# Six of eight groups of an MLP's first half computed transposed, with operands at chosen places

## The chip, the cores and the metric

The kernel runs on one core of a Trainium2 chip. The metric is device time in microseconds (us), from a run's first to its last instruction with what the launch adds around it; lower is better. Engines are named as the profile names them: PE (matrix unit, its weight loads apart as PEld), DVE (vector), ACT (scalar and activation), POOL, and SP, which here only issues DMAs.

## The reference

A decoder trunk of two layers on 256 tokens of 1024 features, float32, batch 1. Each layer is a mixer and an MLP, each between two RMS norms with gains:

```python
for layer in range(2):
    h = rms_norm(x, norm_mix_pre[layer])
    m = mixer_a(h, ...) if layer == 0 else mixer_c(h, ...)
    x = x + rms_norm(m, norm_mix_post[layer])
    h = rms_norm(x, norm_mlp_pre[layer])
    x = x + rms_norm(sq_relu_mlp(h, mlp_w1[layer], mlp_w2[layer]), norm_mlp_post[layer])

def sq_relu_mlp(h, w1, w2):          # w1: 1024 x 4096, w2: 4096 x 1024
    h = jax.nn.relu(h @ w1)
    return (h * h) @ w2
```

Mixer A is a gated short convolution beside latent attention with 8 heads; mixer C is sparse attention with 16 heads in three branches. Both start with a wide input projection and end with an output projection. For the change the MLP matters, and of the mixers only where their matmul operands lie.

## The kernel before, in words

**Precision.** A float32 product is built from three matmuls on rounded operands: both factors are split into a high part, rounded to the format that PE multiplies fast, and a low part, the rest; high x high, high x low and low x high are summed in PSUM (`mm3`, L119). Weights come by DMA in chunks of 128 x 1024 (512 KB, tile `raw`); `chunk` (L158) lets ACT copy the high part (`whi`, L177, two halves of 512) and DVE subtract for the low part (`wlo`, L178). Five chunk buffers (`WB`) hold split weights; a side pool of three (`xhi`, `xlo`) takes the first chunks of the next stage. All this runs ahead of PE.

**A group** (`group_steps`, L199) is 512 output columns. The activations stand: for a token tile t (two of 128 tokens) and a slice kt of 128 features, the 128x128 block of x transposed (`xth`, `xtl`) is loaded as weights, and 512 columns of `whi` or `wlo` move through. 8 slices x 3 products = 24 matmuls per token tile, first all of t = 0, then all of t = 1: "half groups" below. Tokens lie on PSUM's partitions.

**The MLP** (`mlp`, L340). The first half has 8 groups (j = 0 to 7). When a half group ends, `epi_for` (L346) lets ACT apply ReLU with the token's 1/rms as scale (tile `hr`, L349), DVE square it (`hs`, L351), and, 3.5 us later by the planner's clock, PE transpose it in four blocks of 128x128 (`tr`, L111), since the second half needs the hidden values with their features on the partitions. ACT copies the high part from PSUM (`hh`, L359), DVE subtracts for the low one (`hl`, L360). The second half (`two_sided`, L305) has 32 slices of 128 hidden features, 2 column groups and 2 token tiles: 32 x 2 x 2 x 3 = 384 matmuls of 512 columns, `hh` and `hl` standing. `finish` (L273) then computes the norm behind it (ACT `sq` L278, DVE `pst` L280, POOL `rp` L147), adds to X (L287) and sets off the transposes of X for the next stage (`transposed`, L255), which make the four `xth`/`xtl` pairs, one per token tile and half of the features.

**What sets the order.** PE's order is fixed by the program: a small planner (`tick`, `defer`, L74 to L89) adds an estimate per matmul to a clock and lets deferred work, such as transposes and attention heads, into PE's stream when it comes due. The other engines' orders are a scheduler's; they work in order, each instruction waiting by semaphores. DMAs are all issued by SP.

**Places.** By the addresses that the build gives to the tiles, modulo 128 bytes (a standing block and its moving columns; difference = standing minus moving; "within 512" where it tells more):

| stage, matmul width | moving | standing | difference |
|---|---|---|---|
| MLP first half, 512 | whi, wlo: 64 | xth, xtl: 0 | 64 |
| MLP second half, 512 | whi, wlo: 64 | hh, hl: 64 | 0 (0 within 512) |
| a_in, c_in (input projections), c_out, 512 | whi, wlo: 64; xhi, xlo: 96 | xth, xtl: 0 | 64; 32 |
| a_out, 512 | whi, wlo: 64 | 96 | 32 |
| a_kv 512, a_qup 384 | whi, wlo: 64 | 32 | 96 |
| a_c, first use of 256 | xhi, xlo: 96 | 0 | 32 |
| c_v1, 256 | whi, wlo: 64 | 0 | 64 |
| scores in mixer C, 256 or 512 | kTh, kTl: 96 | qT: 96 | 0 (384 within 512) |

Of the kernel before, what the change touches and what calls it, by code (L numbers as in the profile page):

```python
# [17 lines left out]
P = 128  # L18
# [25 lines left out]
FILL = (900.0, 1400.0, 1200.0, 800.0, 900.0, 1200.0, 900.0, 900.0, 1000.0, 1100.0, 1300.0, 1400.0)  # L44


class Pairs:


    def __init__(self, tiles, t, q):  # L50
        self.tiles, self.t, self.q = tiles, t, q

    def __getitem__(self, key):
        i = 4 * self.q + key[1]
        return self.tiles[i // 2][:, 2 * (i % 2) + self.t, :]


class Trunk:
# [43 lines left out]

    def mm(self, ps, a, b, start, stop, passes=1):
        self.nc.tensor.matmul(ps, a, b, start=start, stop=stop)  # L104
        n = 1
        for d in b.shape[1:]:
            n *= d
        self.tick(passes * max(25.0, n / 2.4 + 2.5))
# [45 lines left out]

    def close_extra(self):
        self.xs.close()

# [82 lines left out]

    def xt_tile(self, part):
        return self.mp.tile([P, 4, P], F32R, name="xt" + part, tag="xt" + part, bufs=4)

# [10 lines left out]

    def transposed(self, src, gcols, res, q, new=None, n=4):  # L255

        new = new or self.xt_tile
        h, l = new("h"), new("l")
# [13 lines left out]

    def finish(self, t, ps, ms, cg, gp, idx, x, rx):  # L273

        nc = self.nc
        with self.tc.high_priority():
            sl = slice(cg * 512, (cg + 1) * 512)
            nc.scalar.activation(self.scratch("sq"), ps, AF.Square, scale=1.0 / 32.0, accum_out=ms[:, cg:cg + 1])  # L278
            tmp = self.scratch("pst")
            nc.vector.tensor_tensor(tmp, ps, gp[:, sl], op=OP.mult)  # L280
            self.tmp.append(tmp)
            if cg == 0:
                return
            r = self.rstd_of((ms[:, 0:1], ms[:, 1:2]), EPS, "rp")
            for i in range(2):
                sl = slice(i * 512, (i + 1) * 512)
                nc.vector.scalar_tensor_tensor(self.X[t][:, sl], self.tmp.pop(0), r, self.X[t][:, sl],  # L287
                                               OP.mult, OP.add)
# [50 lines left out]

    def mlp(self, layer, x, rx, fin):  # L340
        nc, A = self.nc, self.A
        with self.pool("hid") as hp:
            gp = self.gain_post(2 * layer + 1)
            hid = [[None] * 8 for _ in range(2)]

            def epi_for(j):  # L346
                def epi(t, ps):
                    r = hp.tile([P, 512], F32, name="hr", tag="hr", bufs=2)
                    nc.scalar.activation(r, ps, AF.Relu, scale=self.rxof(rx, t))  # L349
                    s = hp.tile([P, 512], F32, name="hs", tag="hs", bufs=3)  # L350
                    nc.vector.tensor_tensor(s, r, r, op=OP.mult)  # L351

                    def later():
                        pt = self.trp()
                        for i in range(4):
                            self.tr(pt[:, i, :], s[:, i * P:(i + 1) * P])
                        h = hp.tile([P, 4, P], F32R, name=f"hh{t}_{j}")
                        l = hp.tile([P, 4, P], F32R, name=f"hl{t}_{j}")
                        nc.scalar.activation(h, pt, AF.Copy)  # L359
                        nc.vector.tensor_tensor(l, pt, h.bitcast(F32), op=OP.subtract)  # L360
                        hid[t][j] = (h, l)
                    self.defer(3500.0, later)
                return epi

            self.first_two(self.group_steps(x, f"w1_{layer}", 0, 8, 512, epi_for(0), 0, cs=self.ahead),
                           self.group_steps(x, f"w1_{layer}", 1, 8, 512, epi_for(1), 1))
            for j in range(2, 8):
# [5 lines left out]
            self.two_sided(hid, f"w2_{layer}", 32, lambda *a: fin(*a, gp),  # L373
                           ahead=ahead if layer == 0 else None)


    def mixer_a(self, x, rx, fin):
        nc, A = self.nc, self.A
        with ExitStack() as st:
# [17 lines left out]
            with self.pool("lc") as cpool:  # L397
                cqs = [cpool.tile([P, 768], F32, name=f"cqs{t}") for t in range(2)]
                ckvs = [cpool.tile([P, 256], F32, name=f"ckvs{t}") for t in range(2)]
                cms = [cpool.tile([P, 4], F32, name=f"cms{t}") for t in range(2)]  # L400
                ckvT = [[None], [None]]
                seen = [0]

                def ctile(n):
                    def new(part):
                        seen[0] += 1
                        return cpool.tile([P, n, P], F32R, name=f"ct{part}{seen[0]}")
                    return new
# [216 lines left out]
    def mixer_c(self, x, rx, fin):  # L625
        nc, A = self.nc, self.A
        with ExitStack() as st:
            lp = st.enter_context(self.pool("ca"))
            pp = st.enter_context(self.pool("caps", space=PSUM))
            cbias = lp.tile([P, 2, C_HEADS, 16], F32, name="cbias")  # L630
            has = lp.tile([P, 2], F32, name="has")
            kTh = lp.tile([P, GRP, 2, 2, P], F32R, name="kTh")
# [6 lines left out]
            qT = [[None] * 4 for t in range(2)]  # L639
            gates = [lp.tile([P, 3, C_HEADS], F32, name=f"gates{t}") for t in range(2)]  # L640
            rq = [None, None]
# [145 lines left out]

            mixT = [[None, None], [None, None]]
            ready, out_ps, out_cs = {}, {}, {}
# [126 lines left out]
            def pv_(n):  # L916
                for _ in range(min(n, len(pvq))):
# [7 lines left out]
                    if last:  # L925
                        mh, ml = self.xt_tile("h"), self.xt_tile("l")
                        m2 = mh.rearrange("p a b -> p (a b)")
                        y = yps[gp, t]
                        nc.scalar.activation(m2, y, AF.Copy)
                        nc.vector.tensor_tensor(ml.rearrange("p a b -> p (a b)"), y, m2.bitcast(F32),  # L930
                                                op=OP.subtract)
                        mixT[t][gp] = (mh, ml)
# [69 lines left out]
    def start(self, x):  # L1002
# [7 lines left out]
        for _ in range(WARM):  # L1010
            nc.tensor.matmul(ps, warm[:, 0:P], warm, start=True, stop=True)
        hs, ls = [], []
        for t in range(2):
            for q in range(2):
                x[t][q] = Pairs(hs, t, q), Pairs(ls, t, q)
        with self.pool("init") as ip:
            raw = ip.tile([P, 8, 2, P], F32, name="x0r")

            def part(i):
                sl = slice(2 * i, 2 * i + 2)  # L1020
                nc.sync.dma_start(raw[:, sl], A["xT"][:, sl])
                h, l = self.xt_tile("h"), self.xt_tile("l")
                hs.append(h)
                ls.append(l)
                self.split_scaled_([(h[:, 2 * k:2 * k + 2], l[:, 2 * k:2 * k + 2], raw[:, 2 * i + k],
                                     self.cols[:, 2 * i + k:2 * i + k + 1]) for k in range(2)])
            part(0)
# [6 lines left out]
            cs.append(self.chunk(W[0, 3], 2, 512))  # L1034
        c2 = []
        for t in range(2):
            c2.append(self.chunk(A["a_c"][0, t], 4, 256, extra=True))
# [6 lines left out]
    def run(self):  # L1044
# [11 lines left out]
        with self.tc.manual_schedule(engines={mybir.EngineType.PE}):  # L1056
            for layer in range(2):
                for part in range(2):
                    idx = 2 * layer + part + 1
                    nx, nrx = [[None, None], [None, None]], [None, None]  # L1060

                    def fin(t, ps, ms, cg, gp, idx=idx, nx=nx, nrx=nrx):
                        self.finish(t, ps, ms, cg, gp, idx, nx, nrx)
                    if part == 1:
                        self.mlp(layer, x, rx, fin)
# [4 lines left out]
                    x, rx = nx, nrx  # L1070

# [102 lines left out]
```

## Time and profile before

| what | value |
|---|---|
| median of 3 runs | 653.75 us (653.66 to 654.86) |
| the profiled execution | 654.89 us, its span 652.9 us |
| granted clock of PE, mean | 0.994 |
| busy: PE, PEld, DVE, ACT, POOL | 638.5, 515.8, 417.7, 382.8, 77.8 us |
| matmuls and weight loads | 3150 each |
| moved by DMA | 110.04 MB, mean 169 GB/s |

In the span, layer 0's mixer ends at about 129 us, its MLP at 309; layer 1's mixer at 461, its MLP at 653. How to read it: a row of the chain of waits or of the timeline gives start, length, engine, line, tiles (out <- in) and count; a row of groups gives count, busy us, mean ns, then the idle time before and what ended it. Matmuls overlap, so the pace of a stream is the distance between starts, or a chain piece's length over its count, and not the length of one matmul's record (0.39 us for 512 columns, 0.28 us for 256). A few per cent of the records can be missing.

### The profile page before, as it was taken

The page shows a single profiled execution, that of the slowest core. Times are in us where ns is not written, and L with a number is a line of the kernel's source. Part 1 is how long each engine was busy: PE and PEld are TensorE (multiplying, and loading weights), DVE is VectorE, ACT ScalarE, POOL GpSimd, SP SyncE. Part 2 cuts the span into 40 slices and gives each one's busy share as a digit, 9 for nine tenths or more (in the row PEclk, how much of TensorE's full clock was granted, in tenths as well). Part 3 has the DMA queues.
Part 4 walks back from the last instruction along what each step waited for, and adds up shares of the span by engine and source line. Part 5 has one row for each costly group of instructions (what it writes and reads, how often), then busy time and mean ns, then how long its engine had stood idle before and what let it go on. Part 6 is the DMA issues. An engine that isn't in the chain of part 4 may idle for free.

```text
span 652.9 us, 9401 instructions
## 1 busy us (share of the span) xinstructions
PE 638.5 (98%) x3150; PEld 515.8 (79%) x3150; DVE 417.7 (64%) x963; ACT 382.8 (59%) x866; POOL 77.8 (12%) x135
## 2 busy tenths in 40 slices
PE   8999999999999999999999999999999999999995
PEld 4889877788888888888889876566788888888884
DVE  6668798766657654447748787754965665644443
ACT  4886566746556544446737778765855655644431
POOL 1202340020000000000200155640200000000000
PEclk9999999999999999999999999989999999999998
DMA  8856346545644665556615734012645565655521
GB/s 274 285 188 224 110 123 204 204 141 161 194 162 162 202 212 195 195 184 237 209 34 162 261 102 155 33 65 79 212 141 181 160 192 165 211 194 194 192 79 64
DMA packets 32608, 110.04 MB, mean 169 GB/s; under 512 B 4080, under 2 KB 4656, under 8 KB 32560
## 3 DMA queue, kind: packets, MB, share of 16 engines
q1 hardware_dynamic: 32560, 109.44, 51.3%
q8 instruction: 25, 0.41, 0.3%
q14 instruction: 23, 0.19, 0.1%
HBM read 108.38 MB, written 1.05 MB: 168 GB/s over the span
## 4 chain that ended last, share of the span: by engine, by line
PE 93%; DVE 2%; issue 1%; ACT 1%; DMA 1%; SPq 0%; POOL 0%; DVEq 0%; POOLq 0%; ACTq 0%
PE acc L104 80%; PE tr L111 6%; PE sc L104 5%; DMA raw<-in_a_in 1%; PE tr L116 1%; PE yp L104 1%; ACT pbn L875 1%; DVE xlo L178 0%; DVE wlo L178 0%; ACT pt L899 0%; DVE X L287 0%; POOL rp L147 0%; DVE pbn L873 0%; DVE pst L280 0%; ACT whi L177 0%
## 5 line engine op out<-in xcount | busy, mean ns | idle before, releaser
L178 DVE TENSOR_TENSOR wlo<-raw,whi 128x512 fp32r<-128x512 f32 (+3 forms) x368 | 236.3, 681 | 99.6 <-ACT whi L177 96.4
L177 ACT ACTIVATE whi<-raw 128x512 fp32r<-128x512 f32 (+3 forms) x362 | 205.7, 614 | 106.9 <-PE acc L104 103.2
L104 PE MATMUL acc<-whi,xtl 128*128 128x512 f32 (+3 forms) x416 | 163.5, 393 | 0.0
L104 PE MATMUL acc<-whi,xth 128*128 128x512 f32 (+3 forms) x416 | 161.9, 389 | 0.1
L104 PE MATMUL acc<-wlo,xth 128*128 128x512 f32 (+3 forms) x416 | 160.6, 387 | 1.1 <-DVE wlo L178 1.1
L104 PE MATMUL acc<-whi,hl 128*128 128x512 f32 x256 | 100.0, 391 | 0.0
L104 PE MATMUL acc<-wlo,hh 128*128 128x512 f32 x256 | 99.6, 389 | 0.0
L104 PE MATMUL acc<-whi,hh 128*128 128x512 f32 x256 | 99.6, 389 | 0.0
L104 PEld LDWEIGHTS acc<-whi,xth 128*128 128x128 f32 x416 | 78.5, 189 | 17.4 <-issue 2.8
L104 PEld LDWEIGHTS acc<-wlo,xth 128*128 128x128 f32 x416 | 78.2, 188 | 17.8 <-DVE wlo L178 2.4
L104 PEld LDWEIGHTS acc<-whi,xtl 128*128 128x128 f32 x416 | 78.6, 189 | 14.4
L104 PEld LDWEIGHTS acc<-wlo,hh 128*128 128x128 f32 x256 | 48.1, 188 | 10.0
L104 PEld LDWEIGHTS acc<-whi,hl 128*128 128x128 f32 x256 | 48.1, 188 | 9.9
L104 PEld LDWEIGHTS acc<-whi,hh 128*128 128x128 f32 x256 | 48.1, 188 | 9.8
L147 POOL TENSOR_TENSOR rp<-mse,mhalf 128x1 f32<-128x1 f32 x8 | 4.8, 597 | 405.3 <-DVE mse L144 405.3
L359 ACT ACTIVATE hh<-tr 128x512 fp32r<-128x512 f32 x32 | 19.1, 598 | 48.6 <-PE tr L111 48.6
L360 DVE TENSOR_TENSOR hl<-tr,hh 128x512 fp32r<-128x512 f32 x32 | 22.1, 692 | 38.5 <-ACT hh L359 38.5
L880 POOL TENSOR_SCALAR pbn<-pbn,sm,gates 128x128 f32<-128x128 f32 (+1 forms) x64 | 37.3, 593 | 77.3 <-DVE sm L877 74.5
L351 DVE TENSOR_TENSOR hs<-hr 128x512 f32<-128x512 f32 x32 | 22.0, 688 | 17.3 <-ACT hr L349 17.3
L875 ACT ACTIVATE pbn<-pbn,nm 128x128 f32<-128x128 f32 (+1 forms) x64 | 28.5, 448 | 7.7 <-DVE nm L873 5.9
L349 ACT ACTIVATE hr<-acc,rx 128x512 f32<-128x512 f32 x32 | 22.0, 688 | 18.6 <-PE acc L104 17.4
L873 DVE CUSTOM_DVE_ANT_0 pbn<-sc,bias 128x128 f32<-128x128 f32 (+1 forms) x64 | 21.2, 348 | 3.3 <-PE sc L104 3.0
(234 smaller groups left out, 777.4 us busy)
## 6 DMA issues: line engine op xcount, KB each, us to landing
raw<-in_w SPq DMA_DIRECT2D x128, 512.0 KB, 3.5
raw<-in_c_in SPq DMA_DIRECT2D x16, 512.0 KB, 4.0
raw<-in_a_in SPq DMA_DIRECT2D x15, 512.0 KB, 4.7
raw<-in_a_out SPq DMA_DIRECT2D x8, 512.0 KB, 3.7
raw<-in_c_out SPq DMA_DIRECT2D x8, 512.0 KB, 3.3
raw<-in_a_qup SPq DMA_DIRECT2D x6, 384.0 KB, 3.5
gpost<-in_gpost SPq DMA_DIRECT2D x4, 512.0 KB, 4.8
bias<-in_bias SPq DMA_DIRECT2D x4, 512.0 KB, 5.7
```

The costliest lines, as they stand in the source:

```text
L104: self.nc.tensor.matmul(ps, a, b, start=start, stop=stop)
L111: self.nc.tensor.transpose(dst, src, self.ident)
L116: self.nc.tensor.transpose(dst.bitcast(F32R), src, self.ident_r)
L177: nc.scalar.activation(hi[:, sl], raw[:, sl], AF.Copy)
L178: nc.vector.tensor_tensor(lo[:, sl], raw[:, sl], hi[:, sl].bitcast(F32), op=OP.subtract)
L349: nc.scalar.activation(r, ps, AF.Relu, scale=self.rxof(rx, t))
L351: nc.vector.tensor_tensor(s, r, r, op=OP.mult)
L359: nc.scalar.activation(h, pt, AF.Copy)
L360: nc.vector.tensor_tensor(l, pt, h.bitcast(F32), op=OP.subtract)
L873: nc.vector.tensor_tensor_reduce(pb[:, sl], sp[:, sl], bias[:, r, 256 - nk:], -1.0, BIG, OP.add, OP.min, nm[:, br:br + 1])
L875: nc.scalar.activation(pb[:, sl], pb[:, sl], AF.Exp, bias=nm[:, br:br + 1], scale=-1.0, accum_out=sm[:, br:br + 1])
L880: nc.gpsimd.tensor_scalar(pb[:, sl], pb[:, sl], sm[:, br:br + 1], gates[t][:, 1 + br, h:h + 1], OP.mult, OP.mult)
```

## The change

Groups 2 to 7 of each MLP's first half are computed transposed (`hidden_steps`): a 128x128 block of `w1` stands, and both token tiles move, 2 x 128 = 256 columns. Hidden features then lie on PSUM's partitions, which is what the second half needs, so these groups have no transposes. A group is 4 chunks x 4 blocks of hidden features x 2 slices x 3 products = 96 matmuls of 256 columns into two PSUM tiles of 512, chunk after chunk, so that each chunk is used once and for both token tiles. `epi_turned` takes a PSUM tile (two blocks, both token tiles) through ReLU, square, high copy and low difference, all 512 wide; high and low parts are now read from SBUF, reordered so that token tiles stand apart.

The 1/rms of a token is a scale per partition only where tokens lie on partitions. So it leaves the ReLU in all eight groups: as relu(r a)^2 = r^2 relu(a)^2 for r > 0, its square `r2` is applied in `finish`, in the square's scale and in the multiplication with the gain, now a scalar_tensor_tensor.

To move both token tiles, `xth` and `xtl` hold both in one tile (`xt_both`), three buffers of 1056 instead of four of 512. The offset of 16 elements in the MLPs (`16 if idx in (1, 3)`) puts these operands 64 bytes past a multiple of 128; some tiles in the pools are padded (`even`, and small tiles made wider), so that every other operand of a rounded matmul starts at a multiple of 128. By the build's addresses:

| stage, width | difference now |
|---|---|
| turned groups, 256 | 64 |
| MLP groups 0 and 1, 512 | 64 as before |
| MLP second half, 512 | 0 (0 within 512) as before |
| a_in, a_kv, a_out, c_in, c_out, 512 | 0 (0, 128, 256 and 384 within 512) |
| a_c, c_v1, a_b, a_qup, 256 to 384 | 0 |
| rounded transposes in mixer C, 128 | 0 (were 96) or 64 (were 32) |

The diff, cut to its core:

```diff
@@ trunk helpers
-    def mm(self, ps, a, b, start, stop, passes=1):
-        self.nc.tensor.matmul(ps, a, b, start=start, stop=stop)
+    def mm(self, ps, a, b, start, stop, passes=1, part=False):
+        self.nc.tensor.matmul(ps, a, b, start=start, stop=stop, **({"skip_group_check": True} if part else {}))
+    def even(self, pool, n):
+        pool.tile([P, n], F32, name="even")
     def close_extra(self):
+        self.even(self.xp, 24)
         self.xs.close()
-    def xt_tile(self, part):
-        return self.mp.tile([P, 4, P], F32R, name="xt" + part, tag="xt" + part, bufs=4)
+    def xt_tile(self, part, off=0):
+        x = self.mp.tile([P, 1024 + 32], F32R, name="xt" + part, tag="xt" + part, bufs=3)
+        return x[:, off:off + 1024].rearrange("p (t i n) -> p t i n", t=2, i=4)
+    def xt_both(self, both, q, t, off=0):
+        if both[q] is None:
+            both[q] = self.xt_tile("h", off), self.xt_tile("l", off)
+        return [a[:, t] for a in both[q]]
@@ finish
-            nc.scalar.activation(self.scratch("sq"), ps, AF.Square, scale=1.0 / 32.0, accum_out=ms[:, cg:cg + 1])
-            nc.vector.tensor_tensor(tmp, ps, gp[:, sl], op=OP.mult)
+            if r2 is None:
+                ...
+            else:
+                nc.scalar.activation(self.scratch("sq"), ps, AF.Square, scale=r2[t][:, 1:2], accum_out=ms[:, cg:cg + 1])
+                nc.vector.scalar_tensor_tensor(tmp, ps, r2[t][:, 0:1], gp[:, sl], OP.mult, OP.mult)
...
-                        x[t], i))
+                        x[t], i, lambda: self.xt_both(both, i, t, 16 if idx in (1, 3) else 0)))
@@ mlp
+    def hidden_steps(self, both, wname, j, epi):
+        cs = self.chunks(wname, j, range(4), 2, 512)
+        ps = [self.acc(i).rearrange("p (a n) -> p a n", a=2) for i in range(2)]
+        for c in range(4):
+            for a in range(4):
+                o = ps[a // 2][:, a % 2]
+                for i in range(2):
+                    kt = 2 * c + i
+                    xh, xl = (m[:, :, kt % 4, :] for m in both[kt // 4])
+                    wh, wl = (w[:, i, a * P:(a + 1) * P] for w in cs[c])
+                    first = kt == 0 and a % 2 == 0
+                    last = kt == 7 and a % 2 == 1
+                    self.mm(o, wh, xh, first, False, part=True)
+                    self.mm(o, wh, xl, False, False, part=True)
+                    self.mm(o, wl, xh, False, last, part=True)
+                if c == 3 and a % 2 == 1:
+                    epi(a // 2, ps[a // 2])
-                    nc.scalar.activation(r, ps, AF.Relu, scale=self.rxof(rx, t))
+                    nc.scalar.activation(r, ps, AF.Relu)
+            def epi_turned(j):
+                ...
+                def epi(b, ps):
+                    r = hp.tile([P, 512], F32, name="hr", tag="hr", bufs=2)
+                    nc.scalar.activation(r, ps.rearrange("p a n -> p (a n)"), AF.Relu)
+                    s = hp.tile([P, 512], F32, name="hs", tag="hs", bufs=3)
+                    nc.vector.tensor_tensor(s, r, r, op=OP.mult)
+                    s4 = s.rearrange("p (a t n) -> p a t n", a=2, t=2)
+                    hb, lb = h[:, 2 * b:2 * b + 2], l[:, 2 * b:2 * b + 2]
+                    nc.scalar.activation(hb, s4, AF.Copy)
+                    nc.vector.tensor_tensor(lb, s4, hb.bitcast(F32), op=OP.subtract)
...
+            for t in range(2):
+                r = self.rxof(rx, t)
+                r2[t] = self.small(2, "r2")
+                nc.vector.tensor_tensor(r2[t][:, 0:1], r, r, op=OP.mult)
+                nc.vector.tensor_scalar(r2[t][:, 1:2], r2[t][:, 0:1], 1.0 / 32.0, None, OP.mult)
             for j in range(2, 8):
-                self.group(x, f"w1_{layer}", j, 8, 512, epi_for(j), j)
+                self.hidden_steps(both, f"w1_{layer}", j, epi_turned(j))
@@ mixers: tiles made wider, and the mixed heads in a tile for both token tiles
-            uT = lp.tile([P, 4, 2 + S], F32, name="uT")
+            uT = lp.tile([P, 4, 8 + S], F32, name="uT")
-            has = lp.tile([P, 2], F32, name="has")
+            has = lp.tile([P, 32], F32, name="has")[:, 0:2]
...
```

Two places show the order of the instructions. The first is PE in the first half of layer 0's MLP, group 2, second token tile, before (out <- moving, standing; a number tells buffers apart; L104 is a matmul, L111 four transposes of the half group before):

```order
L104 MATMUL acc0_1921<-whi_1869,xth_1672 128x512
L104 MATMUL acc0_1921<-wlo_1870,xth_1672 128x512
L104 MATMUL acc0_1921<-whi_1869,xtl_1673 128x512
L104 MATMUL acc0_1921<-whi_1869,xth_1672 128x512
L104 MATMUL acc0_1921<-wlo_1870,xth_1672 128x512
L111 MATMUL tr_1939<-ident_70,hs_1919 128x128 x4
L104 MATMUL acc0_1921<-whi_1869,xtl_1673 128x512
```

and now, at the end of group 2 and the beginning of group 3:

```order
L93 MATMUL acc1_1887<-xth_1585,wlo_1881 128x256
L93 MATMUL acc1_1887<-xth_1585,whi_1880 128x256
L93 MATMUL acc1_1887<-xtl_1586,whi_1880 128x256
L93 MATMUL acc1_1887<-xth_1585,wlo_1881 128x256
L93 MATMUL acc0_2039<-xth_1567,whi_2009 128x256
L93 MATMUL acc0_2039<-xtl_1568,whi_2009 128x256
L93 MATMUL acc0_2039<-xth_1567,wlo_2010 128x256
```

Operands have changed sides, 24 matmuls of 512 became 48 of 256, and no transposes of hs stand between them; 32 sets of four stood there in both layers together, 8 are left (groups 0 and 1).

The second place is ACT at the end of group 2 in the changed kernel (L397 is the ReLU of a PSUM tile, L402 the high copy, L171 the weight copies):

```order
L397 ACTIVATE hr_1981<-acc0_1886 128x512
L402 ACTIVATE hh_2_1852<-hs_1983 128x512
L397 ACTIVATE hr_1999<-acc1_1887 128x512
L171 ACTIVATE whi_2153<-raw_2151 128x512 x2
L402 ACTIVATE hh_2_1852<-hs_2001 128x512
L171 ACTIVATE whi_2161<-raw_2159 128x512 x2
L171 ACTIVATE whi_2169<-raw_2167 128x512 x2
L171 ACTIVATE whi_2177<-raw_2175 128x512 x2
L397 ACTIVATE hr_2125<-acc0_2039 128x512
```

The ReLU of acc1_1887 waits for the last matmul of group 2. The chunk copied right behind it, whi_2153, is the first of group 4: all four of group 3 are copied before. In the kernel before, one ReLU stood at the end of each half group, with two or four weight copies between.

More of the change, by code (lines that the diff above doesn't have):

```diff
@@ L363, in epi_for @@
                 return epi
+            def epi_turned(j):
+                h = hp.tile([P, 4, 2, P], F32R, name=f"hh_{j}")
+                l = hp.tile([P, 4, 2, P], F32R, name=f"hl_{j}")
+                def epi(b, ps):
[8 more added lines that the diff above has]
+                    for t in range(2):
+                        hid[t][j] = (h[:, :, t], l[:, :, t])
+                return epi
             self.first_two(self.group_steps(x, f"w1_{layer}", 0, 8, 512, epi_for(0), 0, cs=self.ahead),
                            self.group_steps(x, f"w1_{layer}", 1, 8, 512, epi_for(1), 1))
+            for t in range(2):
+                r = self.rxof(rx, t)
+                r2[t] = self.small(2, "r2")
+                nc.vector.tensor_tensor(r2[t][:, 0:1], r, r, op=OP.mult)
+                nc.vector.tensor_scalar(r2[t][:, 1:2], r2[t][:, 0:1], 1.0 / 32.0, None, OP.mult)
             for j in range(2, 8):
-                self.group(x, f"w1_{layer}", j, 8, 512, epi_for(j), j)
+                self.hidden_steps(both, f"w1_{layer}", j, epi_turned(j))
             def ahead():
@@ L372, in ahead @@
                 self.ahead = self.chunks("c_in", 0, range(4), 2, 512, extra=XB)
-            self.two_sided(hid, f"w2_{layer}", 32, lambda *a: fin(*a, gp),
+            self.two_sided(hid, f"w2_{layer}", 32, lambda *a: fin(*a, gp, r2),
                            ahead=ahead if layer == 0 else None)
@@ L399, in mixer_a @@
                 ckvs = [cpool.tile([P, 256], F32, name=f"ckvs{t}") for t in range(2)]
-                cms = [cpool.tile([P, 4], F32, name=f"cms{t}") for t in range(2)]
+                cms = [cpool.tile([P, 32], F32, name=f"cms{t}") for t in range(2)]
                 ckvT = [[None], [None]]
@@ L404, in ctile, with new @@
                 def ctile(n):
-                    def new(part):
+                    def new():
                         seen[0] += 1
-                        return cpool.tile([P, n, P], F32R, name=f"ct{part}{seen[0]}")
+                        return [cpool.tile([P, n, P], F32R, name=f"ct{part}{seen[0]}") for part in "hl"]
                     return new
@@ L639, in mixer_c @@
             qT = [[None] * 4 for t in range(2)]
-            gates = [lp.tile([P, 3, C_HEADS], F32, name=f"gates{t}") for t in range(2)]
+            gates = [lp.tile([P, 4, C_HEADS], F32, name=f"gates{t}")[:, 0:3] for t in range(2)]
             rq = [None, None]
@@ L925, in pv_ @@
                     if last:
[L926 to L931, printed above, removed]
+                        mh, ml = self.xt_both(mixed_, gp, t)
+                        y = yps[gp, t].rearrange("p (a b) -> p a b", a=4)
+                        nc.scalar.activation(mh, y, AF.Copy)
+                        nc.vector.tensor_tensor(ml, y, mh.bitcast(F32), op=OP.subtract)
                         mixT[t][gp] = (mh, ml)
@@ L1011, in start @@
             nc.tensor.matmul(ps, warm[:, 0:P], warm, start=True, stop=True)
-        hs, ls = [], []
+        both = [[self.xt_tile(part) for part in "hl"] for _ in range(2)]
         for t in range(2):
             for q in range(2):
-                x[t][q] = Pairs(hs, t, q), Pairs(ls, t, q)
+                x[t][q] = [a[:, t] for a in both[q]]
         with self.pool("init") as ip:
@@ L1021, in part @@
                 nc.sync.dma_start(raw[:, sl], A["xT"][:, sl])
[L1022 to L1026, printed above, removed]
+                self.split_scaled_([tuple(a[:, :, 2 * (i % 2) + k] for a in both[i // 2])
+                                    + (raw[:, 2 * i + k], self.cols[:, 2 * i + k:2 * i + k + 1]) for k in range(2)])
             part(0)
@@ L1035, in start @@
         c2 = []
+        self.even(self.mp, 16)
         for t in range(2):
```

30 lines of the change are left out of this document (13 added, 17 removed).

## The prediction

> **What bounds the kernel now.** I read the page's shares first, then the chain of work that ended last, then the two MLPs in a table of stages, then single instructions of TensorE.
>
> ```profile
> PE 638.5 (98%) x3150; PEld 515.8 (79%) x3150; DVE 417.7 (64%) x963; ACT 382.8 (59%) x866; POOL 77.8 (12%) x135
> PEclk9999999999999999999999999989999999999998
> ...
> PE 93%; DVE 2%; issue 1%; ACT 1%; DMA 1%; SPq 0%; POOL 0%; DVEq 0%; POOLq 0%; ACTq 0%
> ```
>
> A busy share of 98% proves little where matmuls overlap; that 93% of the chain is TensorE, at the full clock, does. Time is won where the stream of matmuls gets shorter. The stages of the MLPs (columns: stretch, its us, busy time and count of PE, PEld, DVE, ACT, POOL, clock, DMA share, GB/s):
>
> ```profile
> 149.40:221.80 72.40, 72.40 (x338) 58.60 (x337) 46.03 (x73) 41.70 (x72) 0.00 (x0) 1.00 0.55 175
> 227.80:308.70 80.90, 80.90 (x358) 66.71 (x356) 42.01 (x67) 37.74 (x68) 1.20 (x4) 1.00 0.62 209
> ...
> 484.00:557.00 73.00, 73.00 (x342) 59.41 (x341) 46.62 (x74) 41.86 (x74) 0.00 (x0) 1.00 0.56 174
> ```
>
> The first row is twelve half groups of the first half of layer 0's MLP, the last the same in layer 1, the middle one the second half. ACT and DVE are busy for under two thirds. The chain in order of time (start, us, what) says how a half group is spent:
>
> ```profile
> 149.47 5.60 PE acc L104 x24
> 155.50 5.60 PE acc L104 x24
> 161.54 5.60 PE acc L104 x24
> ...
> 227.82 80.94 PE acc L104 x357
> ```
>
> Each half group is 24 matmuls of 512 columns in 5.60 us, **233.3 ns** each, and the next begins 6.03 us after the last began: 0.43 us go to something else. The last row is the second half: the same width, the same clock, but 80.94/357 = **226.7 ns** each. The 0.43 us are the transposes (start, us, instruction):
>
> ```profile
> 202.94 0.39 PE L104 MATMUL acc<-wlo,xth 128*128 128x512 f32 x1
> 203.17 0.60 PE L111 MATMUL tr<-ident,hs 128*128 128x128 f32 x4
> 203.52 0.48 PE L104 MATMUL acc<-whi,xtl 128*128 128x512 f32 x1
> 203.84 0.39 PE L104 MATMUL acc<-whi,xth 128*128 128x512 f32 x1
> ```
>
> The four take 0.35 us of the order, and the matmul behind them holds the stream 0.32 us in place of 0.23.
>
> **Part 1, the transposes.** Groups 2 to 7 no longer have them: 6 groups x 2 token tiles x 2 layers = 24 sets, x 0.43 us = **-10.4 us**. Groups 0 and 1 keep theirs. Nothing hid these: they lie in the stream that sets the end.
>
> **Part 2, the turned matmuls.** Removed: 12 groups x 48 = 576 at 233.3 ns, 134.4 us. Added: 12 x 96 = 1152 of 256 columns, each with a weight load of its own. So 116.7 ns is even; what does one cost? Streams of that width stand in the mixers, at their beginning and end:
>
> ```profile
> 19.88 0.28 PE L104 MATMUL acc<-xhi,xth 128*128 128x256 f32 x1
> ...
> 24.02 0.28 PE L104 MATMUL acc<-xhi,xtl 128*128 128x256 f32 x1
> ```
>
> These are 36 matmuls, 35 steps in 4.14 us: 118.3 ns. Their operands lie 32 bytes apart within 128. Another group, 64 bytes apart as the new ones will be:
>
> ```profile
> 372.65 0.28 PE L104 MATMUL acc<-whi,xth 128*128 128x256 f32 x1
> ...
> 373.59 0.28 PE L104 MATMUL acc<-whi,xtl 128*128 128x256 f32 x1
> ...
> 374.99 0.28 PE L104 MATMUL sc<-kTh,qT 128*128 128x256 f32 x1
> 375.11 0.28 PE L104 MATMUL sc<-kTl,qT 128*128 128x256 f32 x1
> 375.23 0.28 PE L104 MATMUL acc<-whi,xth 128*128 128x256 f32 x1
> ...
> 375.70 0.28 PE L104 MATMUL acc<-wlo,xth 128*128 128x256 f32 x1
> ...
> 376.50 0.28 PE L104 MATMUL acc<-whi,xtl 128*128 128x256 f32 x1
> ```
>
> Its first stretch runs at 0.94/8 = 117.5 ns, its last at 0.80/7 = 114.3. The two score matmuls between them read their moving operand in two pieces of 128 columns, as the new ones do (one per token tile), and take 0.12 us, so the cut costs little. I take **114.5 ns**, by the last stretch: the new streams are 96 long and may settle as this one did. That is 131.9 us, **-2.5 us**. The upper bound is the two pieces' 120 ns (138.2 us, +3.8). For the lower: 256 further columns cost at most 226.7 - 114.3 = 112 ns, and a 256-wide matmul without any fixed part takes that (129.0 us, -5.4).
>
> **Part 3, places.** By the build's addresses every operand pair of the second half lies at one place within 128 bytes, now as then, so its 226.7 ns should stay. The first half's lie 64 apart, the mixers' mostly 64 or 32, and all of those run at 233:
>
> ```profile
> 33.94 5.59 PE acc L104 x24
> ...
> 472.38 6.99 PE acc L104 x30
> ```
>
> that is 232.9 ns in layer 0's input projection (64) and 233.0 in the first groups of layer 1's MLP (64). I know nothing else that divides the two paces: load on ACT and DVE is alike in the stages above. The change brings 600 matmuls of 512 columns to one place: 192 of a_in, 24 of a_kv, 96 of a_out, 192 of c_in, 96 of c_out. At 6.6 ns that is 4.0 us if all set the end. In the head stages (96 in layer 0, 144 in layer 1) TensorE also waits for softmax:
>
> ```profile
> 369.00:450.00 81.00, 76.70 (x434) 55.65 (x435) 54.76 (x240) 60.87 (x192) 37.29 (x64) 0.98 0.28 93
> ```
>
> so I count half of these 240, and not the first 36, which wait for their weights: 444 x 6.6 = 2.9 us. I give back 0.3 for narrower matmuls and the rounded transposes, whose places move too with no row that says which way. **-2.6 us**, between 0 (places do nothing, or only a match within 512 bytes helps, which the second half alone has) and -4.0.
>
> The Trainium skill, "TensorE: Matmul & The Clock Gate", section "Step-by-step: what each phase is for", speaks against this part: it says that TensorE has two independent read ports and that "Loading the next tile's weights doesn't steal SBUF read bandwidth from the running matmul". By that rule places cost nothing and part 3 is 0. The trace does not decide it: 226.7 against 233.3 ns at one width and clock speaks for places, but only one stage shows the fast pace.
>
> **Part 4, ACT, DVE and the wait.** A half group leaves these behind, in their own rows:
>
> ```profile
> L360 DVE TENSOR_TENSOR hl<-tr,hh 128x512 fp32r<-128x512 f32 x32 | 22.1, 692 | 38.5 <-ACT hh L359 38.5
> L351 DVE TENSOR_TENSOR hs<-hr 128x512 f32<-128x512 f32 x32 | 22.0, 688 | 17.3 <-ACT hr L349 17.3
> ...
> L349 ACT ACTIVATE hr<-acc,rx 128x512 f32<-128x512 f32 x32 | 22.0, 688 | 18.6 <-PE acc L104 17.4
> ```
>
> Four steps per half, before and after; the copy of the high part now reads SBUF, as the weight copy does:
>
> ```profile
> L177 ACT ACTIVATE whi<-raw 128x512 fp32r<-128x512 f32 (+3 forms) x362 | 205.7, 614 | 106.9 <-PE acc L104 103.2
> ```
>
> so the work on either engine stays within 1 us a layer, and 46.03 of 72.40 us leaves room even if the stage shrinks to 66. The results are ready some 2.7 us after a half (four such rows); the earliest use is the second half of the MLP, and group 7's first use lies 336 matmuls later. The scale by 1/rms moves out of the ReLU into the end of the MLP as one squared factor: four DVE instructions of one column per layer, and at the end a multiplication with one scalar more; the row of that form there takes 1.41/2 = 0.70 us against 0.69 now:
>
> ```profile
> 641.37 0.69 DVE L280 TENSOR_TENSOR pst<-acc,gpost 128x512 f32<-128x512 f32 x1 [2.09 <-ACT sq L278]
> 642.84 1.41 DVE L287 SCALAR_TENSOR_TENSOR X<-pst,rp,X 128x512 f32<-128x512 f32 x2 [0.66 <-POOL rp L147]
> ```
>
> All of that I count at 0. It is hidden by the matmul stream but for the last multiplication. The new wait: on ACT the ReLU of a group's second half stands until TensorE ends the group, and the weight conversions behind it stand too. The order shows that the first of these is a chunk of the group after the next; four chunks, a whole group of 96 x 114.5 ns = 11.0 us, are converted ahead. Without that lead each of the twelve groups would stand for a ReLU, a copy and a subtraction (0.688 + 0.614 + 0.69 = 2.0 us), 24 us in all. DMA must bring a chunk of 512 KB in 2.75 us in place of 3.0; the second half already takes one every 12 x 226.7 ns = 2.72 us, at 209 GB/s.
>
> **The sum.** -10.4 - 2.5 - 2.6 + 0 = -15.5 us. The profiled execution took 654.89 us (span 652.9 and 2.0 around it), 1.14 above the median of the runs shown, 653.75. 653.75 - 15.5 = **638.3 us**.
>
> **The rivals.**
>
> *Places do nothing* (or not at these distances). Then part 3 is 0 and the new stream runs like the quoted stretches on average, 117 ns (134.8 us, +0.4): -10.0, **643.8 us**. For it: the fast pace stands in one stage alone, where operands also match within 512 bytes, and stretches 64 apart ran at 117.5. Against: the 6.6 ns hold through 80 us of it.
>
> *Weight loads come to light.* The loads double in number for the same columns, and the record of one is longer than 114 ns:
>
> ```profile
> L104 PEld LDWEIGHTS acc<-whi,xth 128*128 128x128 f32 x416 | 78.5, 189 | 17.4 <-issue 2.8
> ```
>
> If a long stream fell to one matmul per 189 ns, it would be 1152 x 189 = 217.7 us: +83.3 in place of -2.5, **724 us**. It decides from (134.4 + 10.4 + 2.6)/1152 = 128 ns on: from there the change is slower. Against it: 36 matmuls in a row at 118.3 with the same loads.
>
> *Weights come late.* The lead on ACT melts because copies wait for DVE at the head of the queue: up to 24 us, 638.3 + 24 = **662 us**; from 15.5/12 = 1.3 us a group on nothing is left. Against it: the lead of 11 us and a third of ACT idle.
>
> *Given back.* TensorE arrives earlier in the mixers and waits there longer for softmax, the norms or DMA; a third to two thirds of the gain is lost: about **649 us**.
>
> That the change doesn't do what it says I exclude: the order shows the 24 sets gone and 1152 matmuls in.
>
> **How the numbers follow.** Forecast 60%, own range 634 to 641.5 (parts 2 and 3 at their bounds don't meet); places nothing 27%; weight loads 3%; weights late 5%; given back 5%. The range of 8 in 10, **634 to 647**, holds most of the first two and half of the last. A measurement of this kernel tells about 0.2% (1.3 us) from no change. Faster: 60 + 27 + 5 + 1 of the late weights = 93%; the same 2%; slower 5%.
>
> **What would show it.** The transposes of hs at 32 instead of 128; chain pieces of w1 without 0.43 us gaps; a turned group in 96 x 114.5 = 11.0 us (11.3 with the first rival, over 12.3 if loads show); 226.7 ns in the second half still, and the same in a_in, a_out and c_in if places count, 233 if not. TensorE waiting for whi or wlo at a group's start would be the late weights. I am wrong if the turned stream takes over 120 ns a matmul, or if the mixers' stages grow.

## The result and the profile after

The changed kernel takes **644.34 us** (median of 4 runs, 643.85 to 645.70) beside 654.31 (653.66 to 655.77) for the kernel before on the same chip: ratio 0.9846, 95% interval 0.9824 to 0.9867, so 8.7 to 11.5 us faster. The forecast was 638.3. The time is inside the range of 8 in 10 (634 to 647), outside the likeliest case's own range (634 to 641.5), and within 0.6 us of the first rival's 643.8. As the experiments show, it got there for another reason than that rival's.

The page after, shares and the end of the chain:

```profile
PE 626.1 (98%) x3630; PEld 532.5 (83%) x3630; DVE 418.2 (65%) x971; ACT 379.7 (59%) x866; POOL 78.0 (12%) x135
...
PE 63%; issue 28%; DVE 4%; ACT 2%; DMA 2%; POOL 1%; SPq 0%; DVEq 0%; POOLq 0%; ACTq 0%
```

TensorE still sets the end, with 480 more matmuls and 480 more loads in 12 us less. The 28% of "issue" are no idle time; the chain (start, us, what) loses its track in the turned groups and books a whole MLP so:

```profile
137.37 165.33 issue
...
305.91 5.82 PE acc L93 x25
```

Whoever reads that row alone would look for a stall of 165 us. The table of stretches (columns: stretch, its us, busy time and count of PE, clock, DMA share, GB/s) shows that TensorE did not rest in it; over the whole row, 137.37 to 302.70, it is busy for 165.33 of 165.33 us. First the kernel after, the turned groups and the second half of layer 0, then of layer 1; behind it the kernel before:

```profile
160.00:210.00 50.00, 50.00 (x428) 1.00 0.57 189
230.00:300.00 70.00, 70.00 (x310) 1.00 0.61 203
490.00:540.00 50.00, 50.00 (x428) 1.00 0.55 182
562.00:632.00 70.00, 70.00 (x311) 1.00 0.46 150
```

```profile
160.00:210.00 50.00, 50.00 (x235) 1.00 0.53 169
230.00:300.00 70.00, 70.00 (x311) 1.00 0.59 192
```

From such a row the pace follows: records are longer than the pace, so some that began ahead of the stretch are counted too, 0.28/0.117 = 2.4 of 256 columns and 0.39/0.23 = 1.7 of 512. 50/(428 - 2.4) = **117.5 ns** for a turned matmul, in both layers; 70/(310 - 1.7) = 227.0 for the second half, as before. The rows of one group confirm it (start, us, instruction, in the timeline):

```profile
162.74 0.28 PE L93 MATMUL acc<-xth,whi 128*128 128x256 f32 x1
...
174.01 0.28 PE L93 MATMUL acc<-xth,whi 128*128 128x256 f32 x1
```

96 matmuls in 11.27 us, 117.4 ns. The projections, which the change brings to one place within 128 bytes, did not get faster. In the chain of after, layer 0's a_in (with 7 matmuls of a_kv behind it) and a_out:

```profile
33.95 5.59 PE acc L93 x24
...
104.98 15.12 PE acc L93 x65
```

that is 232.9 and 232.6 ns; a_in took 5.59 for 24 before too. The transposes of the hidden tiles are down to groups 0 and 1:

```profile
L100 PE MATMUL tr<-ident,hs 128*128 128x128 f32 x32 | 4.8, 274 | 0.0
```

So the gain is the transposes, and both other parts of the sum gave nothing. From the first X transposes of a stage to the next stage's first matmul, the first halves of the MLPs shrank by 4.3 and 4.4 us; the second halves shrank by 0.4 and 0.5, for the last set of transposes stood in them before. Layer 1's mixer ran 1.6 us shorter (149.1 to 147.5), but without the pads too, in the first run below, it takes 147.3, and the old profile shows a clock of 0.98 there; I don't count it to the change.

### The profile page after: what moved, and what is told of

Its sections match the earlier page's. It is cut to its first block, busy times and chain, and to the rows that moved or that the text cites. A ratio compares the mean times of both kernels' runs of the same rounds, so it can differ in the third digit from the quotient of the medians.

```text
span 641.9 us, 10332 instructions
## 1 busy us (share of the span) xinstructions
PE 626.1 (98%) x3630; PEld 532.5 (83%) x3630; DVE 418.2 (65%) x971; ACT 379.7 (59%) x866; POOL 78.0 (12%) x135
## 4 chain that ended last, share of the span: by engine, by line
PE 63%; issue 28%; DVE 4%; ACT 2%; DMA 2%; POOL 1%; SPq 0%; DVEq 0%; POOLq 0%; ACTq 0%
PE acc L93 52%; PE sc L93 5%; PE tr L100 4%; DMA X<-in_x 1%; PE tr L105 1%; DMA raw<-in_a_in 1%; DVE wlo L172 1%; DVE xtl L255 1%; PE yp L93 1%; ACT pbn L923 1%; DVE X L293 1%; POOL rp L140 0%; ACT sq L270 0%; DVE xlo L172 0%; DVE pst L283 0%
## 5 line engine op out<-in xcount | busy, mean ns | idle before, releaser
L171 ACT ACTIVATE whi<-raw 128x512 fp32r<-128x512 f32 (+3 forms) x362 | 205.8, 614 | 135.5 <-PE acc L93 89.0
L93 PE MATMUL acc<-xtl,whi 128*128 128x256 f32 x384 | 107.9, 281 | 0.0
L93 PE MATMUL acc<-xth,wlo 128*128 128x256 f32 x384 | 107.5, 280 | 0.0
L93 PE MATMUL acc<-xth,whi 128*128 128x256 f32 x384 | 107.5, 280 | 0.0
L93 PE MATMUL acc<-whi,xth 128*128 128x512 f32 (+3 forms) x224 | 85.6, 382 | 1.1 <-DVE whi L167 1.1
L93 PE MATMUL acc<-wlo,xth 128*128 128x512 f32 (+3 forms) x224 | 84.4, 378 | 1.2 <-DVE wlo L172 1.0
L93 PE MATMUL acc<-whi,xtl 128*128 128x512 f32 (+3 forms) x224 | 85.2, 380 | 0.0
L93 PEld LDWEIGHTS acc<-xth,wlo 128*128 128x128 f32 x384 | 72.6, 189 | 0.0
L93 PEld LDWEIGHTS acc<-xth,whi 128*128 128x128 f32 x384 | 72.1, 188 | 0.1
L93 PEld LDWEIGHTS acc<-xtl,whi 128*128 128x128 f32 x384 | 72.1, 188 | 0.1
L93 PEld LDWEIGHTS acc<-whi,xtl 128*128 128x128 f32 x224 | 42.1, 188 | 6.6
```

The lines of the kernel that those rows point to most:

```text
L93: self.nc.tensor.matmul(ps, a, b, start=start, stop=stop, **({"skip_group_check": True} if part else {}))
L171: nc.scalar.activation(hi[:, sl], raw[:, sl], AF.Copy)
```

## The experiments

All are told with medians; a run of the kernel before stood beside each (653.95 in the first four, 654.59 in the next four, 654.24 in the grids, 654.43 in the last).

**Take the two parts apart.** The turn alone, without pads and offset (`xth` and `xtl` still hold both token tiles):

```diff
-        x = self.mp.tile([P, 1024 + 32], F32R, name="xt" + part, tag="xt" + part, bufs=3)
+        x = self.mp.tile([P, 1024], F32R, name="xt" + part, tag="xt" + part, bufs=3)
-            x[t], i, lambda: self.xt_both(both, i, t, 16 if idx in (1, 3) else 0)))
+            x[t], i, lambda: self.xt_both(both, i, t)))
-        self.even(self.xp, 24)
...
```

> The changed kernel with the places of before: no padding, no offset (whi, wlo at 64 within 128 bytes, xth, xtl at 0, so the turned groups' operands still lie 64 apart; the second half at one place, all others 64, 32 or 96 apart). Theory A (places do nothing, the gain is the transposes'): as the changed kernel, 643.5 to 645.5 us, and 233 ns a matmul in the input projections as before. Theory B (places help, and the gain was given back elsewhere): slower than the changed kernel by the 2.6 us of part 3, about 647 us.

The places alone, the same pads put into the kernel before:

> The kernel before with the padding alone: every rounded matmul of 512 columns has its operands at one place within 128 bytes, those of the MLP's first half and most of the projections (1045 matmuls) even within 512. Theory A: as before, 653.5 to 655 us, 233 ns in the first half. Theory B: 1368 matmuls x 6.6 ns = 9.0 us faster, about 645 us, and 227 ns in the first half.

The offset of the MLPs alone taken out of the change (`16 if idx in (1, 3) else 0` becomes `0`):

> The changed kernel without the offset of 16 elements: the turned groups' operands at one place within 128 bytes instead of 64 apart. Theory A: as the changed kernel, 643.5 to 645.5 us, turned groups at 117 to 118 ns a matmul. Theory B: they run as the scores in two pieces did that lay at one place, 120 ns, 1152 x 2.6 ns = 3 us slower, about 647 us.

Measured: the turn alone **639.72** (ratio 0.9777, 0.9761 to 0.9793), the places alone **650.52** (0.9946, 0.9929 to 0.9963), without the offset **646.07** (0.9874, 0.9856 to 0.9893). So the change does better without its places, by 4.6 us, though places are worth 3.4 us to the kernel before. The theories missed all three times: the turn alone is quicker than both of its theories said, and the other two runs lie between theirs. The turned stretches, of the turn alone and then of the run without the offset:

```profile
160.00:210.00 50.00, 50.00 (x444) 1.00 0.62 193
...
490.00:540.00 50.00, 50.00 (x444) 1.00 0.61 191
```

```profile
160.00:210.00 50.00, 50.00 (x424) 1.00 0.59 188
```

444 against 428 is 113.2 against 117.5 ns. From start to start the mean is 113.4 over all of them; 1152 x (117.5 - 113.4) = 4.7 us covers the difference. Without the offset it is 118.6: 1.3 us more than the change, measured 1.7.

By the build's addresses, one thing divides these three. In the turn alone the gap (standing minus moving) is 64 bytes within 512 for every turned matmul. A tile of 1056 elements, though, is 4224 bytes, 128 more than a multiple of 256; the three buffers lie one behind the other, and the low parts three tiles behind the high ones. In the change the gaps are 192, 320 and 448 within 512, and they alternate from matmul to matmul (192, 64, 192 for the three products of a block, counted within 256, then 64, 192, 64 with the other half of the features). All of them are 64 within 128. Without the offset they are 256, 384 and 0, in the same alternation. In the places alone, most of the first half's pairs are at 0 within 512, and the first half does go faster, 239 and 238 records (its transposes among them) where the kernel before has 235 and 236; a half group takes 5.50 us in its chain, 229.2 ns a matmul, which is less than the 233.3 of before and more than the 227 expected:

```profile
160.00:210.00 50.00, 50.00 (x239) 1.00 0.57 176
...
490.00:540.00 50.00, 50.00 (x238) 1.00 0.53 169
```

In the change the projections' are at 0, 128, 256 and 384.

**Is it the data?** Behind the ReLU many of the second half's standing values are zero; that could explain 226.7 ns as well as a place. The edit: `AF.Relu` becomes `AF.Copy` in both epilogues, so the ReLU is left out.

> The changed kernel without the ReLU (a plain copy stands in its place, so this part of the computation is left out): hidden values are squares without the zeros that the ReLU makes of about half of them. Theory C (the second half runs at 226.7 ns because of its data, half zeros): 233 ns there, 768 x 6.6 ns = 5.1 us slower than the changed kernel, about 649.4 us. Theory B (it is their place within 512 bytes): 226.7 ns and 644.3 us.

Measured 645.09 (0.9864, 0.9845 to 0.9883), and the second half as it was:

```profile
230.00:300.00 70.00, 70.00 (x310) 1.00 0.63 200
```

The data theory falls.

**Places counted within 512.** High and low parts share one tile whose length is a multiple of 512 bytes, so that every buffer stands alike; 16 elements in the MLPs and 32 elsewhere give a gap of 64 to the turned matmuls and 0 to nearly all else (448 to the MLPs' groups 0 and 1). (To make room, the square that nobody reads is written in 16 bits.)

```diff
-        x = self.mp.tile([P, 1024 + 32], F32R, name="xt" + part, tag="xt" + part, bufs=3)
+        x = self.mp.tile([P, 2048 + 128], F32R, name="xt", tag="xt", bufs=3)
+        v = x[:, off:off + 2048].rearrange("p (s t i n) -> p s t i n", s=2, t=2, i=4)
-            16 if idx in (1, 3) else 0
+            16 if idx in (1, 3) else 32
-        self.even(self.xp, 24)
+        self.even(self.xp, 88)
...
```

> The change with its places counted within 512 bytes instead of 128: moving token tiles begin 64 bytes below the standing weights in all turned matmuls, nearly all other operands stand at one place within 512. Theory 'within 512': the turned stream goes at 113.3 ns as with the turn alone, and the projections of the mixers, some 520 matmuls of 512 columns, fall from 232 to between 227 and 229 ns, 1.6 to 2.8 us below the turn alone (639.7): 637 to 638, the quickest of all. Theory 'the places do nothing, the turn alone had luck with its buffers': 639.7 or more, no matter how they stand.

The same with 32 in the MLPs too, so that the turned matmuls' gap is 0:

> As the run before, but the turned operands too at one place within 512 bytes, hi, lo and all buffers alike. Theory 'a gap of 64 bytes is what the turned stream needs': 117 ns or more for each of 1152, 4 to 7 us above the run before (641 to 645). Theory 'what counts is that all pairs stand alike, the gap itself is nothing': 113.3 ns, 637 to 638 as the run before.

Measured **638.17** (0.9741, 0.9715 to 0.9767), the lowest time here, and 645.88 (0.9854, 0.9825 to 0.9883). The first of the two, a_in and a_out in the chain, then its turned stretch in the table:

```profile
33.80 5.50 PE acc L93 x24
...
104.47 14.78 PE acc L93 x65
```

```profile
160.00:210.00 50.00, 50.00 (x444) 1.00 0.58 187
```

The turned stretch with a gap of 0:

```profile
160.00:210.00 50.00, 50.00 (x419) 1.00 0.56 182
...
490.00:540.00 50.00, 50.00 (x419) 1.00 0.59 181
```

a_out goes from 232.6 to 227.4 ns and a_in from 232.9 to 229.2: the places are worth something to the projections, where they are right. By its time, 1.5 us below the turn alone, that would not be clear, since the two intervals touch; the paces carry it. At a gap of 0, uniform as it is, the turned stream takes 50/(419 - 2.4) = 120.0 ns. So the gap matters, and what is best for 512 columns is worst for 256. The theory that only uniformity counts has fallen, and that the turn alone had luck with its buffers too.

**Which period?** The turn alone with the hidden tiles 256 bytes further on (`self.even(hp, 64)` at the pool's start):

> The turn alone, with all tiles of the hidden layer 256 bytes further on: the second half's operands, at one place within 512 before, are at one place within 128 and 256 but not within 512. Theory 'within 512': its 768 matmuls go from 226.7 to about 232.5 ns, 768 x 5.8 = 4.5 us: 644.2. Theory 'within 128' (that of the prediction): 226.7 stays, 639.7.

Measured 640.04 (0.9777, 0.9742 to 0.9812); the second half does not care:

```profile
230.00:300.00 70.00, 70.00 (x310) 1.00 0.68 204
```

So 512 is not the period; 128, that of the prediction, was contradicted by the projections of the change, though those mixed gaps. Three grids settle it: the 512-byte version with other gaps in one stage each (`off` chosen by layer, `self.even(hp, n)` by layer; the side pool's pad stays at 24, so its first chunks stand 256 bytes from where they did).

> The run with both kinds of places (638.2), with other gaps in one stage each, all pairs of a stage alike: turned matmuls 128 bytes apart in layer 0 and 192 in layer 1, the second half's operands 128 apart in layer 0 and 64 in layer 1. Theory 'within 256' (0 and 256 alike, all else bad for 512 columns): both second halves at 232 instead of 226.7, 4 us more; turned at 113.3 only at 64 and 320, so both stages at 117 to 120, 4 to 8 us more: 646 to 650. Theory 'the second half is quick wherever it stands, by something other than its place': 226.7 in both layers, 642 to 646. Theory 'within 128': layer 0's second half at 226.7, its turned ones as at 0, 120.

> The same with turned matmuls 256 bytes apart in layer 0 and 320 in layer 1, the second half's operands 32 apart in layer 0 and 192 in layer 1. Theory 'within 256': turned at 120 in layer 0 as at 0 (576 x 6.6 = 3.8 us more), 113.3 in layer 1 as at 64; second half at 232 in both, 4 us more: 646. Theory 'within 512': turned at neither of these paces; the second half as before. Theory 'not its place': second half at 226.7, 642.

> The same with turned matmuls 448 bytes apart in layer 0 and 384 in layer 1, the second half's operands 384 apart in layer 0 and 320 in layer 1. Theory 'within 256': every stage as in the first of these three with the same gap less 256 (448 as 192, 384 as 128, 320 as 64), 646 to 650 and within 1 us of it. Theory 'within 512': paces that differ from those by over 1 ns for the turned ones. If uniform gaps of 192, 320 and 448 all give 113.3, the changed kernel's 117.4, which mixes these three, comes from the mixing and not from a gap.

Measured 647.82 (0.9909, 0.987 to 0.9948), 645.43 (0.9865, 0.9814 to 0.9916) and 647.85 (0.9901, 0.9871 to 0.9932). Their stretches, in this order of runs: turned and second half of layer 0, then of layer 1.

```profile
160.00:210.00 50.00, 50.00 (x424) 1.00 0.58 188
230.00:300.00 70.00, 70.00 (x303) 1.00 0.59 187
490.00:540.00 50.00, 50.00 (x444) 1.00 0.61 197
562.00:632.00 70.00, 70.00 (x302) 1.00 0.49 158
```

```profile
160.00:210.00 50.00, 50.00 (x419) 1.00 0.57 186
230.00:300.00 70.00, 70.00 (x302) 1.00 0.59 189
490.00:540.00 50.00, 50.00 (x444) 1.00 0.60 191
562.00:632.00 70.00, 70.00 (x307) 1.00 0.47 150
```

```profile
160.00:210.00 50.00, 50.00 (x444) 1.00 0.60 189
230.00:300.00 70.00, 70.00 (x302) 1.00 0.60 195
490.00:540.00 50.00, 50.00 (x423) 1.00 0.56 180
562.00:632.00 70.00, 70.00 (x301) 1.00 0.46 151
```

With the runs above, and as the mean from start to start over each stage, in ns:

| gap of all pairs of a stage, within 512 | 256 columns (turned) | 512 columns (second half) |
|---|---|---|
| 0 and 256 | 120.0 and 120.0 | 226.7 and 226.7 |
| 32 | not tried | 233.3 |
| 64 and 320 | 113.4 and 113.4 | 233.3 and 233.3 |
| 128 and 384 | 118.7 and 118.7 | 232.3 and 233.3 |
| 192 and 448 | 113.6 and 113.6 | 228.9 and not tried |

For the cell not tried, a_in of the turn alone stands at 448; its chain has 24 of its matmuls in 5.49 us, 228.8 ns.

Gaps 256 bytes apart agree, within 0.1 ns at 256 columns and 1.0 at 512; those 128 apart do not (0 and 128 at either width, 64 and 192 at 512): **what counts is the gap within 256 bytes.** "Within 128" and "within 512" have both fallen, and of the theory "within 256" its clause that all gaps but 0 are bad for 512 columns: 192 costs 2.2 ns, and 64 costs 6.6. It is the gap and not the place of one operand: in the turn alone the turned weights start at 64 and the tokens at 0, modulo 512, in the 512-byte version at 128 and 64, and both take 113.4 ns. And uniform gaps of 64 and of 192 give the same 113.5: each of the changed kernel's gaps alone would have been quick.

**Mixing.** What is left for its 117.5 is that they alternate. In the 512-byte version, layer 0's low parts are moved 128 bytes on (gaps 64, 192, 64 within 256 for the three products), in layer 1 the second half of the rows (the gap changes twice per group):

```diff
-            16 if idx in (1, 3) else 32
+            {1: 16, 3: 16 + 32 * i}.get(idx, 32), 32 if idx == 1 else 0
...
```

> The run with both kinds of places (638.2; gaps of 64 bytes in all turned matmuls) with one edit: in layer 0 the low parts of the tokens stand 128 bytes further on than the high parts, so that the gap within 256 bytes alternates between 64 and 192 from matmul to matmul, each of which alone gave 113.4; in layer 1 the second half of the rows (high and low parts alike) stands 128 bytes further on, so that the gap changes twice per group of 96. Theory 'mixing from matmul to matmul is what cost the changed kernel its 4 ns': layer 0 at 117 ns, layer 1 at 113.5, 576 x 3.8 = 2.2 us more, 640.4. Theory 'each pair counts by itself': both layers at 113.4, 638.2, and the changed kernel's 117.4 is left without a cause.

Measured 641.85 (0.9808, 0.9778 to 0.9839), 3.7 us above the version without, where 2.2 were expected:

```profile
160.00:210.00 50.00, 50.00 (x426) 1.00 0.58 183
...
490.00:540.00 50.00, 50.00 (x435) 1.00 0.60 189
```

Layer 0 is at 50/(426 - 2.4) = 118.0 ns, as in the changed kernel: **mixing is its cause**. That mixing always costs is not shown: in the run without the offset, 0 and 128 alternate in the same way, and at 118.6 ns it is no slower than 128 alone (118.7). Layer 1, at 115.6, is not the 113.5 expected, and brings the rest of the 3.7 us. In half groups of 48 at a gap of 64, of 192, of 64:

```profile
489.50:494.90 5.40, 5.40 (x50) 1.00 0.45 144
494.95:500.55 5.60, 5.60 (x50) 1.00 0.73 233
500.60:506.00 5.40, 5.40 (x50) 1.00 0.49 155
```

The same 50 records need 5.40 us and 5.60: 113.4 and 117.6 ns. A gap of 192 runs at 117.6 where a stretch of 64 went before, and at 113.6 where all are alike.

**The price of the transposes.** 24 sets put back into the turn alone:

```diff
+                    def later():
+                        pt = self.trp()
+                        for i in range(4):
+                            self.tr(pt[:, i, :], s[:, i * P:(i + 1) * P])
+                    self.defer(3500.0, later)
```

> The turn alone, with the 24 sets of four transpositions put back into the turned stream, their result read by nobody. Theory 'the sets cost 0.43 us each, as the trace of before has it': 24 x 0.43 = 10.4 us more than the turn alone, 650.1. Theory 'each set also throws the stream that follows it off its pace': turned matmuls at 115 to 117 ns beside the sets, 2 to 4 us more, 652 to 654.

Measured 650.57 (0.9931, 0.9907 to 0.9955). The turn with its second half moved by 256 bytes, which changed nothing, stood beside it on the same chip: 650.57 - 640.04 = 10.5 us, 0.44 per set. The timeline shows one, and how the stream goes on behind it:

```profile
188.17 0.60 PE L100 MATMUL tr<-ident,hs 128*128 128x128 f32 x4
188.52 0.37 PE L93 MATMUL acc<-xth,whi 128*128 128x256 f32 x1
188.72 0.28 PE L93 MATMUL acc<-xtl,whi 128*128 128x256 f32 x1
188.84 0.28 PE L93 MATMUL acc<-xth,wlo 128*128 128x256 f32 x1
```

0.35 us for the four, 0.20 for the next matmul in place of 0.113, then a few of 0.12: the first theory, within 0.1 us of its 10.4.

## Why the prediction was right or wrong

**Part 1 (-10.4 us): right.** The sets put back cost 10.5, and they are all that the change gained.

**Part 2 (-2.5): wrong by 3.5, the term that was mis-sized.** 1152 x 117.5 = 135.4 us against 134.4: +1.0, within the bounds. I read two paces at one gap, 117.5 and 114.3, in the quoted score stage, and took the quick one because a long stream "may settle as this one did". Both paces are real, and a long stream of this gap does settle, at 113.4, where all pairs stand alike. The step that failed is "64 bytes apart as the new ones will be": I took the difference within 128 from the address list, where the high and low parts' 64 and 192 read the same. The gaps within 512 were to be had from the same list before the run.

**Part 3 (-2.6): wrong, about 0.** The mechanism was right: at one clock, width and load, the second half's matmuls take 226.7 or 233 ns by their place, and with the period respected the projections fell to 227 to 229. The period was wrong. In the changed kernel all pairs of a_out stand at 384, that is 128 within 256, for which the grids give 232.3 to 233.3 ns at 512 columns: its 232.6 is that. The gaps of a_in alternate between 0 and 128 within 256; whether the slow gap alone or the mixing too kept it at 232.9 was not told apart. The two chain rows quoted for this part hold a few matmuls of another gap (7 of a_kv in the one, 7 of the side pool in the other), which changes nothing, as all of them ran at 233. The lower case named beside it, that "only a match within 512 bytes helps", was near; 256 suffices. I had put no chance of its own on it.

The Trainium skill, "TensorE: Matmul & The Clock Gate", section "Step-by-step: what each phase is for", gives the two operands independent read ports, and a load that takes no read bandwidth from the running matmul. What the prediction drew from it, that places cost nothing, does not hold here: 120.0 against 113.4 ns and 233.3 against 226.7, with nothing moved but a tile's start. Whether the two reads meet, which is what the sentence denies, no run here shows. That part 3 came to 0, as by that rule, was luck: the places chosen were not the quick ones.

**Part 4 (0): right.** DVE was busy for 418.2 us after 417.7. ACT had less to do, since a ReLU without a scale per token is shorter:

```profile
L397 ACT ACTIVATE hr<-acc 128x512 f32<-128x512 f32 x24 | 14.2, 590 | 4.6 <-PE acc L93 4.6
```

590 ns in place of 688; in groups 0 and 1, where nothing but the scale went, it is 610. The turned groups start every 11.27 us (at 162.74, 174.01, 185.29, 196.56 and 207.83 in layer 0), so the wait of ACT for a group's second half reached nobody.

**The sum** with the measured terms is -10.4 + 1.0 + 0 + 0 = -9.4 us; measured -10.0, interval -8.7 to -11.5. So the time fell inside the range because the range was wide enough to hold the first rival: of three gains one came, a third of the forecast 15.5 us was missing, and the forecast of 638.3 was 6 us too low.

**The rivals.** *Places do nothing* gave the time, 643.8, and the turned stream's 117 ns, with a group in 11.27 us, but its reason fell: places made the kernel before 3.4 us faster and the turned one 4.6 us slower. *Weight loads come to light*, *late* weights and *given back* did not occur: no stream above 120 ns, no turned stretch that waits for weights, and the first halves' gain of 4.3 and 4.4 us is still in the end time. The price named for *given back*, about 649, was at the upper end of its own words: a third to two thirds of 15.5 us give 643.5 to 648.6.

## What to carry to other kernels

Turning a product so that its result has the layout that the next product needs took 24 sets of transposes out of a TensorE that bounds the kernel, and that was the whole gain. When operands are laid out for pace, take the address modulo every power of two that the kernel could feel, for every buffer and both parts, and keep it alike along a stream: here a pad of 128 bytes that kept the rule "within 128" cost 4.6 us against no pad at all. The same gap is not right for every width, and a chain that says "issue" over a long stretch is to be held against the busy counts.

## What the runs showed of the hardware that I had not expected

- The pace of a stream of matmuls, each with its own weight load, depends on the gap between the standing block that is loaded and the moving columns, within 256 bytes: 113.4 to 120.0 ns at 256 columns, 226.7 to 233.3 at 512. Of the gaps tried, 0 is the best for 512 columns and the worst for 256.
- One and the same gap can run at two paces, by what ran before it: 192 at 113.6 ns in a uniform stream and at 117.6 behind a stretch of 64, for 48 matmuls without falling back. What keeps the slow rhythm up is open; that it is two reads meeting in the memory is a thought that no run here tests.
- In the 512-byte version a_in is at 229.2 where the second half, with the same gap of 0, is at 226.7. Its streams are cut by transposes every 24 matmuls, and the timeline shows that behind each cut the stream needs some ten matmuls to settle:

```profile
28.41 0.40 PE L93 MATMUL acc<-wlo,xt 128*128 128x512 f32 x1
...
29.80 0.39 PE L93 MATMUL acc<-wlo,xt 128*128 128x512 f32 x1
...
31.16 0.39 PE L93 MATMUL acc<-wlo,xt 128*128 128x512 f32 x1
...
32.52 0.39 PE L93 MATMUL acc<-wlo,xt 128*128 128x512 f32 x1
```

Behind the cut at 27.5 us, the first two of these rows are six matmuls and 1.39 us apart, 232 ns each; the last two are six matmuls and 1.36 us apart, 227 ns each. At a gap of 64, in the kernel before, no such settling shows: 233 ns from the cut on.
